# Rows 6 and 7 of the output projection ahead of the first feed-forward products, behind the first transposes of x1; two more slots for y in the last head

## The chip, the cores and the metric

The kernel runs on one core of a Trainium2 chip, as one program. The metric is the device time of one execution in microseconds. Before the change the median of three runs is 1173.84 us (1173.09, 1173.84 and one run of 6371.15 that stands apart). The engines are TensorE (PE for its products, PEld for its weight loads), VectorE (DVE), ScalarE (ACT), GpSimd (POOL, hardly used here) and SyncE (SP), which issues all DMAs.

## The reference

One layer of a hybrid block, for one sequence of 1024 positions and a model width of 1024, in float32:

```python
h = hybrid_mixer(x, ...)                  # three branches, concatenated, @ w_out
x = layer_norm(ALPHA * x + h, ln1_g, ln1_b)          # x1
h = jnp.square(jax.nn.relu(x @ w_up)) @ w_down       # feed-forward, width 4096
x = layer_norm(ALPHA * x + h, ln2_g, ln2_b)
...
return jnp.concatenate([y_conv, y_ml, y_da], axis=-1) @ w_out      # end of hybrid_mixer
```

`y_conv` (256 columns) is a causal depthwise convolution of 31 taps with a layer norm; `y_ml` (256 columns) is a chunked mLSTM; `y_da` (512 columns, 4 heads of 128) is differential attention: two softmax maps for each head, one subtracted from the other, times v, with an RMS norm. The part that the change touches is the product of the concatenated branches with `w_out`, its layer norm (x1 is the result), and the start of the feed-forward part.

## The kernel before, in words

**Precision.** Every large product is made of three: an operand is split into a high part (a ScalarE copy to a rounded format) and a low part (a VectorE subtract), and high*high, high*low and low*high are added up in PSUM. `split` (L145) is that pair of instructions. In the profile, `hi` and `lo` are split weights or inputs, `yh` and `yl` a split row block of y, `wth` and `wtl` split attention weights.

**Stages.** First the input projections, with the convolution and the mLSTM beside them; then four heads of attention, one after another; then the feed-forward part as products of a seven-product (Strassen-like) scheme: P1 to P7, over 16 pairs of 128-column blocks of `w_up` (`up(s, p)`, L1100), and after that `w_down`. The sequence is cut in eight blocks of 128 rows, called row 0 to row 7 here (`tb` in the code).

**The output projection** runs in two passes, since the last heads are late. The branch outputs go to eight DRAM tiles `ydram`, one for each 128 columns. The first pass (`row1`) takes column blocks 0 to 4, adds ALPHA*x and leaves its sums in eight tiles `acc`. The second pass (`row2`, L1074) takes blocks 5, 6 and 7, that is heads 1, 2 and 3. For one row, `get_y` (L857) loads three blocks of `ydram` to `yraw` and splits it to `yh` and `yl`; `row` (L872) then makes 18 products of 512 columns (two halves, three blocks, three products each) into two tiles of the PSUM pool `ps_mm`, which has two banks, adds each half to `acc` on VectorE (L893) and normalises the row: L899, L805 to L811, L904. It stores the result to `zdram`.

**The last head.** `attention(3, ..., fill)` works in four groups g of two row blocks. Scores go to the pool `ps_s`, transposed weights and outputs to `ps_t`, four banks and two; they belong to the attention and are given back at L1092, after which the pool `ps_f` has the six banks. In each group `fill(g)` (L1076) places other work: for g = 1, 2, 3 the rows 2g-2 and 2g-1 of the second pass, and at g = 3 also the first half of the transposes of x1. Group g writes 256 rows of `ydram[7]`, so rows 2g and 2g+1 can be loaded after it; rows 6 and 7 only after the whole head.

**x1.** The feed-forward part needs x1 transposed. `x1_half(t4, ...)` (L981) does it for rows 4*t4 to 4*t4+3: 32 transposes of 128x128 on TensorE into eight banks taken two at a time, each bank read out by ScalarE (L994) or VectorE (L996) into the tiles `xr`. `x1_split` makes the split operands B11 and B21 out of the first half; the others (T1 to T4, B22) are sums with the second half. P1 needs B11, P2 needs B21. The second half of the transposes stands behind the products P1 and P2 of pairs 0 and 1 (L1320).

**Weights.** `w_load(s)` loads two tiles of 512 KB of `w_up`, `w_sums(s)` makes sums x and y out of them, `w_split(s, key)` splits w1, x, y or w2. The last head is preceded by `wo2` (the split of w_out blocks 5 to 7), w_load(0), w_sums(0), w_split(0, "w1") and w_load(1) (L1068 to L1073).

**What sets the order.** Instructions get a priority number when they are written down. `lane(k)` (L88) gives numbers from k million on, so a low lane goes first: 1 for loads, splits and evictions, 2 for the attention, 5 for weights, 6 for products of the rows, 7 for the first transposes; code after L1306 counts from 8 million. When the program is built, each engine's instructions are put in one fixed order, by priority among those that can go; at run time each engine follows its order and waits on semaphores. A lower-priority instruction can thus be put ahead of a higher one that cannot go yet.

**Slots.** SBUF is cut in 47 slots of 128 x 1056 float32. The class `Slots` (L54) hands them out first in, first out: `alloc` takes the slot that was given back longest ago, `free` puts one at the end of the queue, in the order of the code. A new tile in a slot must wait until everything that used the old one is done. From L920 on one ring `F` serves weights, y and x1. Slots are counted by the code, so which tile follows which in a slot can be read off by hand. Before the last head F has 23 free slots: wo2 takes nine and gives three back, w_load(0) takes two, w_sums(0) two, w_split(0, "w1") two and gives one back, w_load(1) two. Ten are left for the rows. After the last head the slots of the attention's ring G join F.

Of the kernel before, what the change touches and what calls it, by code (L numbers as in the profile page):

```python
# [10 lines left out]
F32 = mybir.dt.float32  # L11
# [6 lines left out]
P = 128  # L18
# [79 lines left out]
def mixer_block(ctx: ExitStack, tc: tile.TileContext, a: dict, out: bass.AP):  # L98
# [5 lines left out]
    X = Slots(spool, range(0, 16))  # L104
# [3 lines left out]
    lane = Lanes(tc)  # L108
# [5 lines left out]
    def tr(out, in_, k=P):  # L114
        nc.tensor.transpose(out, in_, ident[:k, :k])  # L115

    def load(out, in_):
        nc.sync.dma_start(out=out, in_=in_)
# [36 lines left out]
    ps_mm = ctx.enter_context(tc.tile_pool(name="ps_mm", bufs=2, space=bass.MemoryType.PSUM))  # L155
# [683 lines left out]
    early = [load_split(W, a["w_out"][kb], D) for kb in range(NEARLY)]  # L839
# [10 lines left out]
    acc = []  # L850
    ydv = [y.rearrange("p (t j) -> p t j", j=P) for y in ydram]

    def out_proj(kbs, first, wo, yring):

        n, ys = len(kbs), {}

        def get_y(tb, ln):  # L857
            with ln(1):
                ring = yring(tb)
                raw = ring.alloc(F32, "yraw")  # L860
                for j, kb in enumerate(kbs):
                    load(raw[:, j * P:j * P + P], ydv[kb][:, tb, :])
                yh, yl = ring.alloc(F32R, "yh"), ring.alloc(F32R, "yl")
                split(raw[:, :n * P], yh[:, :n * P], yl[:, :n * P])
                ring.free(raw)
                if first:
                    xa = (W if tb < NW - 2 * NEARLY else X).alloc(F32, "acc")
                    load(xa[:, :D], a["x"][tb])
                    acc.append(xa)
            ys[tb] = ring, yh, yl  # L870

        def row(tb, ahead=(), ln=lane):  # L872
            for t in ahead:
                get_y(t, ln)
            ring, yh, yl = ys[tb]
            mv = small.tile([P, 6], F32, tag="mvf", name="mvf")
            for nh in range(2):
                cs = slice(nh * 512, nh * 512 + 512)
                with ln(6):
                    ps = ps_mm.tile([P, 512], F32, name="mm")  # L880
                    for j in range(n):
                        ks = slice(j * P, j * P + P)
                        h, l = wo[j]
                        mm(ps, yh[:, ks], h[:, cs], j == 0, False)
                        mm(ps, yh[:, ks], l[:, cs], False, False)
                        mm(ps, yl[:, ks], h[:, cs], False, j == n - 1)
                with ln(1):
                    z = acc[tb][:, cs]
                    if first:
                        dve.scalar_tensor_tensor(out=z, in0=z, scalar=ALPHA, in1=ps, op0=ALU.mult,  # L890
                                                 op1=ALU.add)
                    else:
                        dve.scalar_tensor_tensor(out=z, in0=ps, scalar=1.0, in1=z, op0=ALU.mult,  # L893
                                                 op1=ALU.add, accum_out=mv[:, nh:nh + 1])
            ring.free(yh, yl)
            if not first:
                with ln(6):
                    z = acc[tb][:, :D]
                    dve.tensor_scalar(out=mv[:, 5:6], in0=mv[:, 0:1], scalar1=mv[:, 1:2],  # L899
                                      scalar2=-1.0 / D, op0=ALU.add, op1=ALU.mult)  # L900
                    junk = yring(tb).alloc(F32, "junk")
                    row_scale(z, mv, junk[:, :D])
                    yring(tb).free(junk)
                    act.activation(z, z, AF.Identity, scale=mv[:, 2:3], bias=mv[:, 4:5])  # L904
                    load(zdram[tb], z)

        return row

    zdram = [dram.tile([P, D], F32, name=f"z{i}") for i in range(TB)]
    row1 = out_proj([0, 1, 2, 3, 4], True, early, lambda tb: X)  # L910
    for tb in range(TB):
        if tb == 0:
            early += [load_split(X, a["w_out"][kb], D) for kb in range(NEARLY, 5)]
# [6 lines left out]
    F = Slots(spool, [])  # L920
# [24 lines left out]
    def bank(of_mm=False):  # L945

        if of_mm:
            return ps_mm.tile([P, 512], F32, name="mm")
        return ps_f.tile([P, 512], F32, tag="f", name="f", bufs=6)
# [26 lines left out]
    xraw, xq = {}, {}  # L976
# [4 lines left out]
    def x1_half(t4, two_banks):  # L981

        for i in range(2):
            xraw[i, t4] = [F.alloc(F32, "xr") for _ in range(2)]
        for kb in (0, 4, 2, 6):
            t_ = two_banks()
            for k in range(2):
                for j in range(4):
                    tr(t_[k][:, j * P:j * P + P],
                       acc[4 * t4 + j][:, (kb + k) * P:(kb + k) * P + P])  # L990
                o = xraw[kb // 4, t4][kb % 4 // 2][:, css[k]]
                g_, b_ = l1g[:, kb + k:kb + k + 1], col(PC_L1B + kb + k)
                if k == 0:
                    act.activation(o, t_[k], AF.Identity, scale=g_, bias=b_)  # L994
                else:
                    dve.tensor_scalar(out=o, in0=t_[k], scalar1=g_, scalar2=b_, op0=ALU.mult,  # L996
                                      op1=ALU.add)

    def x1_split(name, raw, keep=False):

        xq[name] = [halves_of(t, keep) for t in raw]
# [29 lines left out]
    def w_load(s):  # L1031
        w1, w2 = F.alloc(F32, "w1"), F.alloc(F32, "w2")
        load(w1[:, :1024], a["w_up"][s])
        load(w2[:, :1024], a["w_up"][s + NS])
        wt[s] = dict(w1=w1, w2=w2, kept=False)
# [13 lines left out]
    def w_split(s, key, keep=False):  # L1049
        w = wt[s]  # L1050
        raw = w[key]
        if key == "w2":
            both = F.alloc(F32R, "w2")
            split(raw[:, H1], both[:, H0], both[:, H1])
            F.free(raw)
            w["P4"] = both[:, H0], both[:, H1]
            w["P4t"] = (both,)
            return
        hi, lo = halves_of(raw, keep)
        w["kept"] = keep  # L1060
        n0, n1 = dict(w1=("P1", "P2"), x=("P5", "P6"), y=("P7", "P3"))[key]
        w[n0], w[n1] = (hi[:, H0], lo[:, H0]), (hi[:, H1], lo[:, H1])
        w[dict(w1="P2", x="P5", y="P3")[key] + "t"] = hi, lo
# [4 lines left out]
    with lane(5):  # L1068
        wo2 = [load_split(F, a["w_out"][kb], D, False) for kb in (5, 6, 7)]
        w_load(0)  # L1070
        w_sums(0)
        w_split(0, "w1")
        w_load(1)  # L1073
    row2 = out_proj([5, 6, 7], False, wo2, lambda tb: F)  # L1074

    def fill(g):  # L1076

        if g > 0:
            row2(2 * g - 2, (2 * g - 2, 2 * g - 1))
            row2(2 * g - 1)  # L1080
        if g == 3:
            with lane(7):
                x1_half(0, lambda: [ps_mm.tile([P, 512], F32, name="mm") for _ in range(2)])
                F.free(*acc[0:4])
                x1_split("B11", xraw[0, 0], True)
                x1_split("B21", xraw[1, 0], True)
                w_split(1, "w1", True)

    with lane(2):
        attention(3, neglam, dag, None, fill)  # L1090
# [9 lines left out]
    def up(s, p):  # L1100
        h = hd.setdefault(s, {})
        if p in ("P1", "P2", "P5"):
            h["a" if p == "P1" else "b"] = bank(p != "P1")
        ps = h["a" if p in ("P1", "P6", "P7", "P4") else "b"]
        wh, wl = wt[s][p]
        go = mm_on(p)
        for kb in range(4):
            ks = slice(kb * P, kb * P + P)
            xh_, xl_ = xq[BOF[p]][kb // 2]
            cs = css[kb % 2]  # L1110
            go(ps, wh[:, ks], xh_[:, cs], kb == 0, False)
            go(ps, wh[:, ks], xl_[:, cs], False, False)
            go(ps, wl[:, ks], xh_[:, cs], False, kb == 3)
        w_done(s, p)
        if p == "P1":
            h["hp"] = F.alloc(F32, "hp")
            act.copy(h["hp"][:, H0], ps)
        elif p == "P2":
            add(h["hp"][:, H0], h["hp"][:, H0], ps)
        elif p == "P6":  # L1120
            h["hq"] = F.alloc(F32, "hq")
            act.copy(h["hq"][:, H0], ps)
        elif p == "P5":
            act.copy(h["hq"][:, H1], ps)
        elif p == "P7":
            add(h["hq"][:, H1], h["hq"][:, H1], ps)
        elif p == "P3":
            add(h["hq"][:, H0], h["hq"][:, H0], ps)
        else:
            act.activation(h["hp"][:, H1], ps, AF.Relu)  # L1130
# [177 lines left out]
    def here(k):  # L1308
        return nullcontext()

    w_load(2)
    up(0, "P1")
    up(0, "P2")
    row2(6, (6, 7), here)
    row2(7, (), here)
    w_split(0, "x")
    up(1, "P1")
    up(1, "P2")
# [223 lines left out]
```

## Time and profile before

| | |
|---|---|
| median of the runs | 1173.84 us |
| the profiled execution's own time | 1175.76 us |
| its span | 1173.9 us |
| granted TensorE clock, mean | 0.992 |
| TensorE busy | 1140.2 us (97%) |
| VectorE busy | 833.4 us (71%) |
| ScalarE busy | 578.1 us (49%) |
| DMA | 179.86 MB, mean 153 GB/s |

Times in the profile count from the start of the span. A line of the time order has the start, the duration, the engine, the source line, the operation, what is written and read, the shape, and in brackets the idle time before it and who ended it. In the table of stretches a row gives the busy time of each engine in that stretch, with the number of instructions, then the granted clock (1.00 is full), the share of the DMA engines and GB/s. The last head runs until about 505 us, and the feed-forward products begin at about 523 us.

### The profile page before, as it was taken

Reading aid. Unit: us, or ns where it says so; the run is one execution under the profiler, and the core shown is the slowest. Engines: PE = TensorE matmul, PEld = TensorE weight load, DVE = VectorE, ACT = ScalarE, POOL = GpSimd, SP = SyncE. Lnnn points to the kernel's source line nnn. Section 1 sums busy time; section 2 is a strip of 40 time slices with the busy share of each in tenths; the row PEclk is TensorE's granted clock in tenths of the full one; section 3 lists DMA queues with packets and bytes.
Section 4 is the critical chain, followed back from the end, with each engine's and each line's share of the span. In section 5 each row is a group of like instructions: output and inputs, shape, how many; then the busy total and the mean of one; then the engine's idle time right before and its main releaser. Section 6 shows DMA issues by size and latency. Waiting matters only on the chain.

```text
span 1173.9 us, 14934 instructions
## 1 busy us (share of the span) xinstructions
PE 1140.2 (97%) x5630; PEld 933.9 (80%) x5630; DVE 833.4 (71%) x1243; ACT 578.1 (49%) x934; POOL 0.2 (0%) x4
## 2 busy tenths in 40 slices
PE   8999999999999899889999999999999999999996
PEld 6898778878897787667788888888888878888885
DVE  5999658875756537867987677656489676666586
ACT  5212384475665526686655454545544323344561
POOL 0000000000000000000000000000000000000000
PEclk9999999999999999899999999999999999999998
DMA  7202135444635663420275555633894644343331
GB/s 279 71 11 72 37 90 167 154 138 128 192 104 174 211 184 105 161 117 37 101 284 215 189 212 192 215 117 146 302 357 159 218 160 147 124 142 128 97 119 72
DMA packets 81640, 179.86 MB, mean 153 GB/s; under 512 B 7648, under 2 KB 29216, under 8 KB 81568
## 3 DMA queue, kind: packets, MB, share of 16 engines
q1 hardware_dynamic: 81568, 178.91, 45.0%
q8 instruction: 44, 0.72, 0.3%
q14 instruction: 28, 0.23, 0.1%
HBM read 120.12 MB, written 58.72 MB: 152 GB/s over the span
## 4 chain that ended last, share of the span: by engine, by line
PE 83%; DVE 7%; ACT 4%; DMA 3%; issue 1%; SPq 0%; DVEq 0%; ACTq 0%
PE f L940 31%; PE mm L112 25%; PE mm L940 17%; PE s L112 5%; PE t L112 3%; PE t L115 2%; DVE lo L148 1%; ACT hi L147 1%; DVE pp L744 1%; ACT pp L738 1%; DMA vh<-v 1%; DVE acc L963 1%; ACT pp L743 0%; DMA raw<-in_w_out 0%; DVE nm L736 0%
## 5 line engine op out<-in xcount | busy, mean ns | idle before, releaser
L940 PE MATMUL f<-lo,hi 128*128 128x512 f32 x512 | 201.5, 394 | 1.4 <-DVE lo L148 1.3
L940 PE MATMUL f<-hi 128*128 128x512 f32 x512 | 201.9, 394 | 0.8 <-DVE acc L1243 0.5
L940 PE MATMUL f<-hi,lo 128*128 128x512 f32 x512 | 201.2, 393 | 0.0
L940 PE MATMUL mm<-hi 128*128 128x512 f32 x320 | 126.1, 394 | 0.4 <-ACT hi L147 0.4
L940 PE MATMUL mm<-lo,hi 128*128 128x512 f32 x320 | 125.9, 393 | 0.3 <-DVE lo L148 0.3
L940 PE MATMUL mm<-hi,lo 128*128 128x512 f32 x320 | 126.0, 394 | 0.0
L940 PEld LDWEIGHTS f<-hi 128*128 128x128 f32 x512 | 96.5, 188 | 24.0 <-ACT hi L147 1.2
L940 PEld LDWEIGHTS f<-lo,hi 128*128 128x128 f32 x512 | 96.3, 188 | 24.0 <-DVE lo L148 2.6
L940 PEld LDWEIGHTS f<-hi,lo 128*128 128x128 f32 x512 | 96.1, 188 | 22.1 <-DVE lo L148 0.2
L112 PE MATMUL mm<-xh,hi 128*128 128x512 f32 x240 | 95.8, 401 | 5.9 <-ACT xh L147 5.9
L147 ACT CAST hi<-hraw 128x1024 fp32r<-128x1024 f32 x56 | 58.3, 1049 | 85.4 <-DMA hraw<-h 80.2
L148 DVE TENSOR_TENSOR lo<-hraw,hi 128x1024 fp32r<-128x1024 f32 x56 | 68.2, 1223 | 44.2 <-ACT hi L147 41.9
L112 PE MATMUL mm<-xl,hi 128*128 128x512 f32 x240 | 96.1, 400 | 0.0
L112 PE MATMUL mm<-xh,lo 128*128 128x512 f32 x240 | 96.0, 400 | 0.0
L285 DVE SCALAR_TENSOR_TENSOR cacc<-ypad,pc,cacc 128x1024 f32<-128x1024 f32 x60 | 74.2, 1283 | 0.6
L112 PE MATMUL mm<-hi,xh 128*128 128x256 f32 (+1 forms) x256 | 74.1, 289 | 0.0
L112 PE MATMUL mm<-hi,xl 128*128 128x256 f32 (+1 forms) x256 | 73.2, 286 | 0.0
L112 PE MATMUL mm<-lo,xh 128*128 128x256 f32 (+1 forms) x256 | 73.1, 286 | 0.0
L940 PEld LDWEIGHTS mm<-hi 128*128 128x128 f32 x320 | 60.3, 189 | 14.7 <-ACT hi L147 0.8
L940 PEld LDWEIGHTS mm<-lo,hi 128*128 128x128 f32 x320 | 60.2, 188 | 14.4 <-DVE lo L148 0.7
L940 PEld LDWEIGHTS mm<-hi,lo 128*128 128x128 f32 x320 | 60.1, 188 | 13.7
L147 ACT CAST hi<-B 128x1024 fp32r<-128x1024 f32 x36 | 37.6, 1048 | 53.7 <-PE mm L940 24.9
(282 smaller groups left out, 2319.5 us busy)
## 6 DMA issues: line engine op xcount, KB each, us to landing
hraw<-h SPq DMA_DIRECT2D x56, 512.0 KB, 3.4
w<-in_w_up SPq DMA_DIRECT2D x32, 512.0 KB, 4.1
B<-in_w_down SPq DMA_DIRECT2D x32, 512.0 KB, 4.7
h<-hp SPq DMA_DIRECT2D x16, 512.0 KB
h<-hx SPq DMA_DIRECT2D x16, 512.0 KB, 3.0
h<-hq SPq DMA_DIRECT2D x16, 512.0 KB, 3.3
raw<-in_wfm SPq DMA_DIRECT2D x14, 512.0 KB, 3.5
qk<-th SPq DMA_DIRECT2D x8, 512.0 KB
```

The costliest lines, as they stand in the source:

```text
L112: return nc.tensor.matmul(out, lhsT=lhsT, rhs=rhs, start=start, stop=stop)
L115: nc.tensor.transpose(out, in_, ident[:k, :k])
L147: act.copy(hi, src)
L148: dve.tensor_tensor(out=lo, in0=src, in1=hi.bitcast(F32), op=ALU.subtract)
L285: dve.scalar_tensor_tensor(out=av, in0=yp[:, i:i + S], scalar=col(PC_DWW + 31 * c + i), in1=av, op0=ALU.mult, op1=ALU.add)
L738: act.activation(pp[m][:, 0:nk], s_[:, 0:nk], AF.Exp, bias=nm[:, m:m + 1], accum_out=sm[:, m:m + 1])
L744: dve.scalar_tensor_tensor(out=pp[0][:, 0:nk], in0=pp[0][:, 0:nk], scalar=sm[:, 0:1], in1=pp[1][:, 0:nk], op0=ALU.mult, op1=ALU.add)
L940: return nc.tensor.matmul(out, lhsT=lhsT, rhs=rhs, start=start and not more, stop=stop and not more, skip_group_check=more)
L963: dve.tensor_tensor(out=out, in0=p, in1=q, op=ALU.add)
```

## The change: what it does

- `get_y` is cut in two: `fetch` takes the slot and issues the three loads of `yraw`; `get_y` takes the slots of `yh` and `yl` and splits, and fetches first if that was not done. `out_proj` returns `fetch` and `get_y` beside `row`.
- `w_load(1)` no longer stands before the last head but in `fill(3)`, still in lane 5. Twelve slots of F are free for the rows at the start of the head, in place of ten.
- The first transposes of x1, the splits of B11 and B21 and the split of w1 of pair 1 leave `fill(3)`. They stand behind the last head, in the code that counts from 8 million, and the transposes use the six banks of `ps_f` (L949) in place of the two of `ps_mm`.
- The order behind the head was: w_load(2), P1 and P2 of pair 0, rows 6 and 7 with their loads. It is now: loads of y for rows 6 and 7, the transposes, the splits of y for rows 6 and 7, the splits of B11 and B21, w_load(2), row 6, the split of w1 of pair 1, row 7, P1 and P2 of pair 0.

No product, DMA or elementwise instruction is added or removed.

```diff
@@ out_proj
-        def get_y(tb, ln):
+        def fetch(tb):
+            ring = yring(tb)
+            raw = ring.alloc(F32, "yraw")
+            for j, kb in enumerate(kbs):
+                load(raw[:, j * P:j * P + P], ydv[kb][:, tb, :])
+            return ring, raw
+
+        def get_y(tb, ln, fetched=None):
             with ln(1):
-                ring = yring(tb)
-                raw = ring.alloc(F32, "yraw")
-                for j, kb in enumerate(kbs):
-                    load(raw[:, j * P:j * P + P], ydv[kb][:, tb, :])
+                ring, raw = fetched or fetch(tb)
                 yh, yl = ring.alloc(F32R, "yh"), ring.alloc(F32R, "yl")
...
-        return row
+        return row, fetch, get_y
...
         w_load(0)
         w_sums(0)
         w_split(0, "w1")
-        w_load(1)
-    row2 = out_proj([5, 6, 7], False, wo2, lambda tb: F)
+    row2, fetch_y, get_y = out_proj([5, 6, 7], False, wo2, lambda tb: F)
...
         if g == 3:
-            with lane(7):
-                x1_half(0, lambda: [ps_mm.tile([P, 512], F32, name="mm") for _ in range(2)])
-                F.free(*acc[0:4])
-                x1_split("B11", xraw[0, 0], True)
-                x1_split("B21", xraw[1, 0], True)
-                w_split(1, "w1", True)
+            with lane(5):
+                w_load(1)
...
+    last_y = [fetch_y(tb) for tb in (6, 7)]
+    x1_half(0, lambda: (bank(), bank()))
+    F.free(*acc[0:4])
+    for tb, fetched in zip((6, 7), last_y):
+        get_y(tb, here, fetched)
+    x1_split("B11", xraw[0, 0], True)
+    x1_split("B21", xraw[1, 0], True)
     w_load(2)
+    row2(6, (), here)
+    w_split(1, "w1", True)
+    row2(7, (), here)
     up(0, "P1")
     up(0, "P2")
-    row2(6, (6, 7), here)
-    row2(7, (), here)
     w_split(0, "x")
     up(1, "P1")
```

More of the change, by code (lines that the diff above doesn't have):

```diff
@@ L905, in row @@
                     load(zdram[tb], z)
-        return row
+        return row, fetch, get_y
     zdram = [dram.tile([P, D], F32, name=f"z{i}") for i in range(TB)]
-    row1 = out_proj([0, 1, 2, 3, 4], True, early, lambda tb: X)
+    row1, _, _ = out_proj([0, 1, 2, 3, 4], True, early, lambda tb: X)
     for tb in range(TB):
```

## The prediction

> **What bounds the kernel now.** I read the page first, then a table of stretches, then the instructions of TensorE in order of time around the change, and last who ended its waits.
>
> ```profile
> span 1173.9 us, 14934 instructions
> PE 1140.2 (97%) x5630; PEld 933.9 (80%) x5630; DVE 833.4 (71%) x1243; ACT 578.1 (49%) x934; POOL 0.2 (0%) x4
> ...
> PE 83%; DVE 7%; ACT 4%; DMA 3%; issue 1%; SPq 0%; DVEq 0%; ACTq 0%
> ```
>
> TensorE is busy for 97% of the span and carries 83% of the chain that ended last. The change removes no product, so it can win only idle or slowed time of TensorE. The next table (start:end and length, then busy us and instructions of PE, PEld, DVE, ACT, POOL, then the granted clock) says where that is.
>
> ```profile
> 480.00:500.00 20.00, 16.18 (x75) 13.05 (x74) 17.17 (x36) 12.93 (x25) 0.00 (x0) 0.83 0.38 115
> 500.00:515.00 15.00, 15.00 (x67) 12.06 (x66) 9.88 (x33) 11.51 (x23) 0.00 (x0) 1.00 0.31 122
> 515.00:530.00 15.00, 11.46 (x60) 8.29 (x59) 10.87 (x22) 13.24 (x20) 0.00 (x0) 1.00 0.26 106
> 530.00:545.00 15.00, 15.00 (x67) 12.13 (x66) 6.87 (x21) 7.33 (x13) 0.00 (x0) 1.00 0.09 36
> 545.00:590.00 45.00, 43.01 (x197) 33.43 (x195) 44.22 (x52) 31.54 (x39) 0.00 (x0) 1.00 0.28 102
> 590.00:1160.00 570.00, 569.48 (x2466) 463.34 (x2465) 397.12 (x466) 258.45 (x306) 0.00 (x0) 1.00 0.51 180
> ```
>
> From 590 on there is nothing to win: 569.48 of 570 us. There are three places: A, the end of the last head (480 to 500: 3.8 us idle, clock 0.83); B, the first transposes of x1 (515 to 530: 3.5 us idle); C, 545 to 590, with 2.0 us idle where VectorE is full (44.22 of 45).
>
> **Place A.**
>
> ```profile
> 489.74 0.39 PE L112 MATMUL mm<-hi,yl 128*128 128x512 f32 x1
> 492.21 1.44 PE L115 MATMUL t<-cst,pp 128*128 128x128 f32 x8 [2.08 <-DVE pp L744]
> 494.24 0.58 PE L112 MATMUL t<-wth,vh 128*128 128x256 f32 x1 [0.59 <-DVE wtl L148]
> 499.42 0.54 PE L112 MATMUL mm<-hi,yh 128*128 128x512 f32 x1
> ...
> 482.59 1.22 DVE L148 TENSOR_TENSOR lo<-raw,hi 128x1024 fp32r<-128x1024 f32 x1
> 483.83 1.28 SPq L118 DMA_DIRECT2D yraw<-ydram  x3
> 491.98 1.22 DVE L148 TENSOR_TENSOR lo<-w,hi 128x1024 fp32r<-128x1024 f32 x1
> 494.16 0.52 ACT L147 CAST yh<-yraw 128x384 fp32r<-128x384 f32 x1
> 494.91 0.55 DVE L148 TENSOR_TENSOR yl<-yraw,yh 128x384 fp32r<-128x384 f32 x1
> 495.37 1.22 DVE L148 TENSOR_TENSOR lo<-wx,hi 128x1024 fp32r<-128x1024 f32 x1
> ```
>
> Row 1 of the second output projection ends at about 489.97, and TensorE stands still until the attention's last transposes; row 2, the work that could stand there, comes only at 499.42. Its y arrives late because of the ring of slots, which is first in, first out: counted through the code, row 2 gets for yraw the slot of the third w_out raw (split until 483.81, loads at 483.83) and for yh the slot of w1 of pair 0, read until 493.20 by the subtract at 491.98. So yh is written at 494.16.
>
> With w_load(1) gone from before the head, the ring holds 12 free slots in place of 10. Counted again, row 2's yraw, yh and yl get the three w_out raws' slots, all free at 483.81, so its y can be whole by about 486, in time for 489.97. Row 3 pays: its yraw now gets the slot of w1, free at 493.20.
>
> What the gap cost, from rows of normal speed:
>
> ```profile
> 473.53 0.34 PE L112 MATMUL t<-wth,vh 128*128 128x256 f32 x1
> ...
> 475.63 0.45 PE L112 MATMUL mm<-lo,yh 128*128 128x512 f32 x1
> ...
> 517.58 1.09 PE L115 MATMUL mm<-cst,acc 128*128 128x128 f32 x8 [0.46 <-DVE acc L893]
> ...
> 531.36 8.12 PE mm L112 x35
> ...
> DMA to landing us min/median/max: 1.9/2.9/3.4
> ```
>
> Between 473.53 and 475.63 lie 18 products of weights and values, 2.10 us, so the 24 of the last group are worth 2.80; eight transposes 1.09; a row product is 8.12/35 = 0.232, a row of 18 takes 4.18. From 489.97 to 499.42 pass 9.45 us for 1.09 + 2.80: 5.56 are lost, 2.67 as idle and the rest to a slow clock. Afterwards: row 2 until 494.15, transposes until 495.24, the wait for wtl (0.59, kept at 0.6), products until 498.64. Row 3 then starts 4.96 us ahead of 503.60, where row 2 ended before. Row 3's y: slot at 493.20, last of three loads issued 0.85 later, landed 2.9 later, copies 0.52 and 0.55: 498.0, a margin of 0.6. VectorE now has row 2's subtract and eviction around that split of w1, so I take a stall of 0.4. **A: 4.6 gained**, bounds 0 (the order stays) and 5.56.
>
> The clock, row first:
>
> ```profile
> 490.00:492.50 2.50, 0.42 (x4) 0.32 (x4) 2.50 (x5) 0.42 (x1) 0.00 (x0) 1.00 0.66 239
> 492.50:495.00 2.50, 1.91 (x11) 1.51 (x9) 2.33 (x6) 1.91 (x4) 0.00 (x0) 0.55 0.23 61
> 495.00:497.50 2.50, 2.50 (x14) 2.50 (x13) 1.74 (x3) 2.50 (x7) 0.00 (x0) 0.50 0.01 1
> ```
>
> A gap of 2.08 us was followed by about 5 us at half clock. [...]
>
> **Place B.** Before, the first transposes pass through two banks of ps_mm behind row 5, nothing else is ready, and the first product waits for the splits of B11.
>
> ```profile
> 516.52 0.60 PE L115 MATMUL mm<-cst,acc 128*128 128x128 f32 x4
> ...
> 520.70 1.09 PE L115 MATMUL mm<-cst,acc 128*128 128x128 f32 x8 [0.91 <-DVE xr L996]
> ...
> 524.51 0.51 PE L940 MATMUL f<-lo,hi 128*128 128x512 f32 x1 [0.77 <-DVE lo L148]
> ...
> 544.84 3.84 PE L115 MATMUL f<-cst,acc 128*128 128x128 f32 x28
> ...
> 593.99 2.77 PE mm L940 x12
> ```
>
> From 516.52 to 544.84, where the second transposes begin, pass 28.32 us. The work in them: 32 transposes at 3.84/28 = 4.39 (the second set, with six banks, shows this pace), rows 6 and 7 with 36 x 0.232 = 8.35, four products of 12 at 2.77 = 11.08; 23.82 in all, so 4.50 are lost. Afterwards the transposes have the six banks that the attention gave back, and rows 6 and 7, 8.35 us, lie over the splits of B11 and B21 (eight instructions) and of w1 of pair 1. Are these covered?
>
> ```profile
> 508.38 0.69 DVE L893 SCALAR_TENSOR_TENSOR acc<-mm,acc 128x512 f32<-128x512 f32 x1
> ...
> 511.30 0.56 DVE L148 TENSOR_TENSOR yl<-yraw,yh 128x384 fp32r<-128x384 f32 x1
> ...
> 513.50 1.24 ACT L904 ACTIVATE acc<-acc,mvf 128x1024 f32<-128x1024 f32 x1 [1.53 <-DVE mvf L811]
> ...
> 519.84 0.81 DVE L996 TENSOR_SCALAR xr<-mm,l1g,pc 128x512 f32<-128x512 f32 x1 [0.75 <-PE mm L115]
> ...
> 523.23 1.23 DVE L148 TENSOR_TENSOR lo<-xr,hi 128x1024 fp32r<-128x1024 f32 x1
> ```
>
> Row 3 is normalised 513.50 + 1.24 - 508.38 = 6.4 us after its last eviction began, and rows 4 and 5 cover 8.35. B11 and B21 cost VectorE 4 x 1.23 = 4.9 against that 8.35, with four evictions of rows 6 and 7 at 0.69: 7.7, just covered. The new exposed step is y of rows 6 and 7. Their raws are fetched early, but yl of row 6 takes the slot of row 5's yh, free only when row 5 ends, and stands behind the evictions of the transposes if the order follows the code. Then the last eviction (0.81) and yh (0.52) leave TensorE dry for 1.3 us; but before, row 6's y was subtracted at 511.30, well ahead of its place in the code (behind the first products), so a subtract can be slipped in where VectorE is free, and I take half, 0.7. **B: 3.8 gained**, bounds 0 and 4.50.
>
> **Place C and the queues.** The split of x of pair 0 was done before 500 (lo<-wx at 495.37); the ring now hands it the slot of acc0, so it runs after the transposes, 1.23 of VectorE more there, with 1.1 for y of rows 6 and 7 just before. The 8.1 us that VectorE sits idle between 530 and 545 take this first; what spills into 545 to 590 delays TensorE one for one. I take 0.5 lost; bounds 2.3 lost (all of it) and 2.0 gained (C's idle gone, since row 7 ends about 5.5 us of products earlier against the second transposes). w_load(1) is two DMAs of 512 KB; they now wait for row 2's junk and row 3's yh, and their w1 is first split behind row 6, some 17 us later (rows 4 and 5, transposes, row 6: 8.35 + 4.39 + 4.18), against this time to landing of 4.1:
>
> ```profile
> w<-in_w_up SPq DMA_DIRECT2D x32, 512.0 KB, 4.1
> ```
>
> So they cost nothing unless SP stands still. On SP, row 3's loads now wait at the head for the w1 slot; queued behind are the loads for rows 4 and 5, which need row 0's and row 1's junk anyway, and the store of the last y group. The six loads of rows 6 and 7 have rows 4 and 5 and the transposes, 8.35 + 4.39, over them.
>
> **The sum.** 4.6 + 3.8 - 0.5 = 7.9. The profiled execution took 1175.76, with 1.86 outside the span, and would take 1167.9; the median of the runs shown, 1173.84, becomes **1165.9, say 1166**.
>
> **Rivals.** (1) Only B is won: row 2 keeps its place, because the order on TensorE is fixed when the program is built. Against it: its y is ready 8 us sooner. 1173.84 - 3.3 = 1170.5; chance 0.16. (2) Only A is won: y of rows 6 and 7 opens a gap of 2 us or more, the clock halves, and the 24 products that took 5.18 in place of 2.80 (494.24 to 499.42) price that at 2.4: B's gain is gone, 1169.7; 0.12. (3) The 32 transposes do not hold the clock up: the run of 4.39 us would be followed by one drop, 2.4 more, 1168.3. The table has clock 1.00 over 515 to 530 with 32 of them and little else for 6 us, so 0.04. [...] (4) The change does not do what it says: as row 6's subtract at 511.30 shows, instructions were already moved against the code's order, and the new order may come out much like the old. 1173.5; 0.08. (5) Slower: SP stands at row 3's loads because the subtract of w1 falls behind row 2's evictions on VectorE, which themselves wait for TensorE. Each us beyond the margin of 0.6 costs one, and 2.4 more once the gap passes 2 us. A's 4.96 and the 3.3 of B and C are used up when it starts after about 498.5, in place of 491.98; at 502 the result is 1177.3. For it: the split is queued below everything of the attention. Against it: its inputs are there, and VectorE was not full over that stretch (17.17 of 20). 0.08.
>
> **How the numbers follow.** The forecast has 0.50 and its own range 1163 to 1169. Rivals 1 to 4 lie below 1174, 0.40 together. The range 1162.5 to 1174 has at the lower end all of A, all of B and 1.3 of C; it leaves out rival 5 and a remainder of 0.02. About 2%, 23.5 us, is what a measurement of this kernel can tell from no change. The idle time of all three places is 9.4, so faster by 2% has 0.01; slower by 2% would need three times rival 5, 0.02; within 2% 0.97.
>
> **What would show it.** Right: no gap above 1 us on TensorE between row 1's end and the last head's end, clock 1.00 there, row 2's products ahead of the last weights-and-values products; the first transposes at one pace on bank f, then rows 6 and 7 at once, then the first product with no wait on lo. Wrong: a wait of row 3's products for yl, a clock below 1 after a new gap, SP idle behind a yraw load, or more than 2.5 us idle from 540 to 585.

## The result and the profile after

The changed kernel takes 1168.43 us (median of four runs, 1167.34 to 1169.96) against 1173.54 for the kernel before (also four runs, with the one of 6371.15 among them): a ratio of 0.995, 95% interval 0.9938 to 0.9962. The interval leaves the run that stands apart out, and is 4.5 to 7.3 us, 5.9 in the middle. The profiled execution took 1168.21.

The first lines of the page of the kernel after, with its chain by engine:

```profile
span 1166.4 us, 14925 instructions
PE 1136.2 (97%) x5630; PEld 930.8 (80%) x5630; DVE 830.8 (71%) x1243; ACT 577.5 (50%) x934; POOL 0.2 (0%) x4
...
PE 85%; DVE 7%; DMA 3%; ACT 3%; issue 2%; SPq 0%; DVEq 0%; ACTq 0%
```

TensorE's busy time fell by 4.0 us with the same 5630 products, mostly since products at half clock last longer: the last 24 products of weights and values took 5.18 us before (494.24 to 499.42) and take 2.78 here (491.20 to 493.98), and the clock of 480 to 500 went from 0.83 to 1.00, which is (1.00 - 0.83) x 20 = 3.4; the rest of what the span lost is idle time. The chain has TensorE at 85% where it had 83%. The span is 7.5 us shorter, which is more than the runs give. Part of it is not the change's. One product of the order in time shows it; the order of the instructions of TensorE, VectorE and ScalarE ahead of it is the same in both kernels. TensorE in the kernel before, with the product near 582 that waits for `hq` behind place C:

```profile
390.34 0.76 PE L112 MATMUL mm<-hi,yh 128*128 128x512 f32 x1 [2.75 <-DVE tl L148]
...
582.65 0.47 PE L940 MATMUL f<-hi,w 128*128 128x512 f32 x1 [0.66 <-DVE hq L963]
```

The same product in the kernel after:

```profile
388.01 0.77 PE L112 MATMUL mm<-hi,yh 128*128 128x512 f32 x1 [2.48 <-DVE tl L148]
```

It starts 2.33 us sooner in the execution after. Over the twelve traces of this study its start spreads from 388.01 to 390.34. All comparisons of traces below therefore count from this product. From it, the second transposes of x1 begin 148.67 us later (536.68) where it was 154.50 (544.84): 5.8 gained. Up to the product that waits for `hq` (574.16 and 582.65) it is 6.2.

The same stretches as before, in the kernel after (busy us and instructions of PE, PEld, DVE, ACT, POOL, then granted clock, DMA share, GB/s):

```profile
480.00:500.00 20.00, 17.62 (x94) 13.79 (x95) 15.80 (x35) 12.55 (x25) 0.00 (x0) 1.00 0.27 92
500.00:515.00 15.00, 14.99 (x77) 12.32 (x77) 9.64 (x38) 12.45 (x23) 0.00 (x0) 1.00 0.72 237
515.00:530.00 15.00, 13.45 (x60) 10.71 (x61) 14.87 (x32) 14.16 (x21) 0.00 (x0) 1.00 0.18 73
530.00:545.00 15.00, 14.99 (x82) 12.42 (x81) 9.21 (x16) 11.19 (x18) 0.00 (x0) 1.00 0.18 72
545.00:590.00 45.00, 43.21 (x183) 33.57 (x182) 42.80 (x52) 27.71 (x34) 0.00 (x0) 1.00 0.37 134
```

The clock is 1.00 throughout, and 515 to 530 has 1.6 us idle where it had 3.5. But 480 to 500 is still 2.4 us idle. TensorE in order of time says where:

```profile
480.51 0.50 PE L112 MATMUL mm<-lo,yh 128*128 128x512 f32 x1 [1.40 <-DVE lo L148]
482.33 0.96 PE L115 MATMUL t<-cst,pp 128*128 128x128 f32 x7 [0.62 <-DVE sm L741]
484.10 0.50 PE L112 MATMUL mm<-lo,yh 128*128 128x512 f32 x1 [0.34 <-DVE lo L148]
485.62 0.50 PE L112 MATMUL mm<-hi,yh 128*128 128x512 f32 x1 [0.33 <-DVE acc L897]
...
491.20 0.29 PE L112 MATMUL t<-wth,vh 128*128 128x256 f32 x1
...
493.98 0.44 PE L112 MATMUL mm<-hi,yl 128*128 128x512 f32 x1
...
498.99 0.88 PE L115 MATMUL f<-cst,acc 128*128 128x128 f32 x6 [0.55 <-ACT acc L908]
499.72 0.50 PE L112 MATMUL mm<-hi,yh 128*128 128x512 f32 x1
...
504.00 0.82 PE L115 MATMUL f<-cst,acc 128*128 128x128 f32 x6
...
512.96 2.57 PE L115 MATMUL f<-cst,acc 128*128 128x128 f32 x20
...
518.02 0.50 PE L112 MATMUL mm<-hi,yl 128*128 128x512 f32 x1 [1.55 <-DVE yl L148]
...
536.68 3.98 PE L115 MATMUL f<-cst,acc 128*128 128x128 f32 x32
...
574.16 0.47 PE L944 MATMUL f<-hi,w 128*128 128x512 f32 x1 [0.61 <-DVE hq L967]
```

The gap of 2.08 us ahead of the last transposes of the attention is gone: row 2 now stands there, on both sides of the last 24 products of weights and values (491.20 to 493.98). Two things are new. Idle time now lies some 10 us earlier, where row 0 of the second pass waits for the splits of w_out (1.40 and 0.34, the `lo`) and around them. And 12 of the 32 first transposes no longer stand behind row 5: six are put after row 2 and six after row 3 (498.99 and 504.00). They are those of rows 0 and 1, one for each of the six banks. Why they fit there, VectorE's instructions say, in order of time:

```profile
492.16 1.22 DVE L148 TENSOR_TENSOR lo<-w,hi 128x1024 fp32r<-128x1024 f32 x1
493.29 0.33 DVE L903 TENSOR_SCALAR mvf<-mvf 128x1 f32<-128x1 f32 x2
...
497.46 0.56 DVE L148 TENSOR_TENSOR yl<-yraw,yh 128x384 fp32r<-128x384 f32 x1 [0.69 <-ACT yh L147]
...
498.97 0.69 DVE L897 SCALAR_TENSOR_TENSOR acc<-mm,acc 128x512 f32<-128x512 f32 x1 [0.95 <-ACT acc L908]
...
503.77 0.69 DVE L897 SCALAR_TENSOR_TENSOR acc<-mm,acc 128x512 f32<-128x512 f32 x1 [1.46 <-ACT acc L908]
```

ScalarE's normalisation of row 1, in the kernel after:

```profile
502.51 1.23 ACT L908 ACTIVATE acc<-acc,mvf 128x1024 f32<-128x1024 f32 x1
```

SP's queue in the kernel after, whose first loads of y for row 3 are among these nine:

```profile
493.45 4.88 SPq L118 DMA_DIRECT2D yraw<-ydram  x9
```

An eviction is VectorE's addition of a finished half row to `acc`. The first one of row 3 (503.77) starts when the normalisation of row 1 ends (502.51 + 1.23 = 503.74), though the two touch different rows of `acc`. What they share is the small tile `mvf` for a row's sums: its pool has two buffers, so row t takes the one of row t-2. While the eviction waits, the two banks of `ps_mm` are full, and the rows' products wait too. The transposes on six banks of their own can go in that time. That row 2 waits in the same way (498.97) has a second side: the last eviction of row 0 ended at 486.17, but VectorE begins row 0's normalisation only at 493.29, in the place that the fixed order gives it. No run here put it earlier.

### The profile page after: what moved, and what is told of

Its sections match the earlier page's. It is cut to its first block, busy times and chain, and to the rows that moved or that the text cites. A ratio compares the mean times of both kernels' runs of the same rounds, so it can differ in the third digit from the quotient of the medians.

```text
span 1166.4 us, 14925 instructions
## 1 busy us (share of the span) xinstructions
PE 1136.2 (97%) x5630; PEld 930.8 (80%) x5630; DVE 830.8 (71%) x1243; ACT 577.5 (50%) x934; POOL 0.2 (0%) x4
## 4 chain that ended last, share of the span: by engine, by line
PE 85%; DVE 7%; DMA 3%; ACT 3%; issue 2%; SPq 0%; DVEq 0%; ACTq 0%
PE f L944 32%; PE mm L112 26%; PE mm L944 17%; PE s L112 5%; PE t L112 3%; PE t L115 2%; DVE lo L148 1%; DMA kh<-qk 1%; ACT pp L738 1%; DVE acc L967 1%; DMA xraw<-in_xT 0%; DMA vh<-v 0%; DMA hraw<-h 0%; DVE nm L736 0%; DVE pp L744 0%
```

## The experiments

Each ratio is against the kernel before, on the same chip, with its 95% interval. Four points cut each trace in three stretches: the product at 390, the end of row 5's products, the beginning of the second transposes, and the first product that waits for `hq` (574.16 in after). The first stretch holds place A, the second is place B, the third is what place C delays. Where 12 transposes lie ahead of row 5's end, 1.65 us (12 x 4.39/32, the prediction's price) is moved from the first stretch to the second. No kernel here leaves computation out.

### The slots alone

```diff
-        w_load(1)                      # before the last head
     def fill(g):
...
         if g == 3:
+            with lane(5):
+                w_load(1)
             with lane(7):
                 x1_half(0, ...)        # transposes, splits stay as before
```

> Only the slots: w_load(1) moves into the third group's fill, so the rows of the last head find 12 free slots in place of 10; the first transposes, and rows 6 and 7, stay where they were. As forecast (place A alone, 4.6 us): about 1169. By the traces of before and after, in which 2.3 of the 7.5 us that separate the two profiles lie ahead of any changed instruction and a new wait of 1.4 us for a split of w_out stands at 480: 2.5 to 3 us, about 1170.5. If the slots do nothing by themselves and the order behind the head did it all: 1173.5. Clock between 490 and 500 us: 1.00 by the first two, about 0.66 by the last.

Measured: 0.9995 (0.9986 to 1.0003), 0.6 us. TensorE in this kernel, in order of time:

```profile
482.20 0.50 PE L112 MATMUL mm<-lo,yh 128*128 128x512 f32 x1 [1.39 <-DVE lo L148]
...
501.43 0.50 PE L112 MATMUL mm<-hi,yh 128*128 128x512 f32 x1 [1.28 <-DVE acc L893]
...
507.10 0.51 PE L112 MATMUL mm<-hi,yh 128*128 128x512 f32 x1 [1.22 <-DVE acc L893]
```

VectorE at the first of the two waits, and below it the normalisation on ScalarE:

```profile
500.68 0.69 DVE L893 SCALAR_TENSOR_TENSOR acc<-mm,acc 128x512 f32<-128x512 f32 x1 [0.95 <-ACT acc L904]
```

```profile
499.40 1.24 ACT L904 ACTIVATE acc<-acc,mvf 128x1024 f32<-128x1024 f32 x1
```

The slots do what the prediction said: no gap at 490, and the clock over 480 to 500 is 1.00 in place of 0.83. But two new waits of 1.28 and 1.22 us stand behind it, and the eviction that ends the first, row 2's, begins when the normalisation of row 0 ends (499.40 + 1.24). Here nothing else is ready for TensorE, so 2.5 us go back. The trace gives 0.63 for place A, 0.05 for B.

### The rows alone

```diff
         w_split(0, "w1")
+        w_load(1)                      # as in the kernel before: ten slots
...
-        if g == 3:
-            with lane(5):
-                w_load(1)              # the rest of the change stays
```

> Only the order behind the head: transposes on six banks, then rows 6 and 7, then the first products; w_load(1) is back in front of the last head, so the rows have 10 slots as before. As forecast (B and C, 3.3 us): 1170.2. By the trace of after (28.3 us between row 5's end and the second transposes became 25.4): 3 us, 1170.5. If the two parts need each other: 1173. The gap of 2 us at 490 and the clock of about 0.66 between 490 and 500 should be there again.

Measured: 0.9953 (0.994 to 0.9966), 5.5 us: nearly the whole change. Its stretch at the end of the head, and TensorE:

```profile
480.00:500.00 20.00, 17.34 (x86) 13.09 (x85) 16.81 (x37) 12.89 (x26) 0.00 (x0) 0.91 0.25 88
```

```profile
483.92 0.96 PE L115 MATMUL t<-cst,pp 128*128 128x128 f32 x7 [2.56 <-DVE sm L740]
...
501.83 0.88 PE L115 MATMUL f<-cst,acc 128*128 128x128 f32 x6 [0.83 <-ACT acc L908]
...
520.71 0.50 PE L112 MATMUL mm<-hi,yl 128*128 128x512 f32 x1 [1.28 <-DVE yl L148]
```

The gap of 2 us at 490 was expected to be there again. With ten slots, as before, it is gone as well. A gap of 2.56 us stands at 484 in its place, and the clock over 480 to 500 is 0.91, where the kernel before had 0.83, so place A still gains 1.75 by the trace. That is the difference of the clock: (0.91 - 0.83) x 20 = 1.6. The head's instructions were not edited. With the work of lane 7 gone from `fill(3)` the fixed order inside the head came out otherwise (on VectorE the sums `wy` of pair 0 now stand ahead of the split of w_out); that the one caused the other is argued, not shown.

### y of rows 6 and 7 ahead of the transposes

```diff
     last_y = [fetch_y(tb) for tb in (6, 7)]
+    for tb, fetched in zip((6, 7), last_y):
+        get_y(tb, here, fetched)
     x1_half(0, lambda: (bank(), bank()))
     F.free(*acc[0:4])
-    for tb, fetched in zip((6, 7), last_y):
-        get_y(tb, here, fetched)
```

> The changed kernel with one step exchanged: the splits of y of rows 6 and 7 stand ahead of the first transposes in the code, so that they are put ahead of the transposes' evictions on VectorE. In the changed kernel TensorE waits 1.55 us for the low part of row 6's y. If that subtract is late only because of the four evictions in front of it: the wait is gone, 1.5 us faster than the changed kernel, about 1167. If VectorE, full in that stretch (14.87 of 15 us), only passes the delay on to the splits of B11 and B21: the same as the changed kernel, 1168.4. If its slots or loads hold it: the same too, with the wait still named yl.

Measured: 0.9931 (0.9919 to 0.9943), 8.1 us, about 2 better than the change, though the two intervals overlap at the edge (0.9938 to 0.9943). The stretch that held the wait for yl:

```profile
515.00:530.00 15.00, 15.00 (x67) 12.16 (x66) 14.71 (x32) 14.05 (x25) 0.00 (x0) 1.00 0.18 71
```

TensorE is full there. Place B gains 4.8 in place of 2.95. In the changed kernel the subtract for row 6 stands behind the evictions of the transposes, as these lines of VectorE in the kernel after show:

```profile
514.34 0.80 DVE L1000 TENSOR_SCALAR xr<-f,l1g,pc 128x512 f32<-128x512 f32 x1
...
515.13 2.24 DVE L1000 TENSOR_SCALAR xr<-f,l1g,pc 128x512 f32<-128x512 f32 x3
...
517.41 0.56 DVE L148 TENSOR_TENSOR yl<-yraw,yh 128x384 fp32r<-128x384 f32 x1
```

Four evictions stand ahead of it, and row 6 cannot go on before it. VectorE works without a break from 512.79 to that subtract, so it is its order that made row 6 wait; with y first no wait for yl is left on TensorE.

### The transposes through two banks

```diff
-    x1_half(0, lambda: (bank(), bank()))
+    x1_half(0, lambda: (bank(True), bank(True)))     # the two banks of ps_mm
```

> The changed kernel with the first transposes passed through the two banks of ps_mm, as before the change, in place of six of ps_f. If the six banks carry part of the gain of place B: the waits for evictions among the transposes come back, 2.3 us in the trace of before (0.46, 0.47, 0.91, 0.43), so about 1170.7. If rows 6 and 7 behind the transposes carry it all, because ScalarE and VectorE are the limit there: 1168.4.

Measured: 0.9977 (0.9967 to 0.9987), 2.7 us: more than half of the gain is lost. TensorE in this kernel:

```profile
500.53 0.50 PE L112 MATMUL mm<-hi,yh 128*128 128x512 f32 x1 [1.28 <-DVE acc L897]
...
514.33 1.27 PE L115 MATMUL mm<-cst,acc 128*128 128x128 f32 x8 [0.41 <-DVE acc L897]
...
518.20 2.99 PE L115 MATMUL mm<-cst,acc 128*128 128x128 f32 x16 [0.91 <-DVE xr L1000]
```

The wait of 1.28 for the eviction is bare again, as with the slots alone, and the transposes wait for their own evictions once more. Six banks thus pay twice: at the transposes, and ahead of them by letting twelve go early. For the second, the bare waits speak (1.28, and 0.37 at 505.34, in place of 0.55); of the 1.7 us that place A loses against the change in the table below, a drop of the clock at 482 (shown at the end) would by itself make up as much.

### Six buffers for the rows' sums: with the slots alone, with the kernel before

```diff
-            mv = small.tile([P, 6], F32, tag="mvf", name="mvf")
+            mv = small.tile([P, 6], F32, tag="mvf", name="mvf", bufs=6)
```

The same in the other two places that use the tag.

> The slots alone again (w_load(1) late, order behind the head as before), and the tile mvf of a row's sums and factors gets six buffers in place of two. With the slots alone the gap of 2 us at 490 was gone and TensorE then stood 1.28 and 1.22 us at 501 and 507 behind evictions that begin when ScalarE's L904 of the row two before ends: the two buffers of mvf. If that is what gave the gain of place A back: both waits gone, 2.5 to 3 us faster than before, ratio about 0.9975. If ScalarE and VectorE are simply late there: ratio 0.9995 as with the slots alone, and the evictions wait for something else.

> The kernel before, with six buffers of mvf and nothing else changed: the control for the slots with six buffers (ratio 0.9963). If the two buffers matter only once row 2 can start at 490, because before that the rows run without a wait: ratio 1.000. If the buffers alone gave that gain: 0.9965.

Measured: slots with buffers 0.9963 (0.995 to 0.9976), 4.3 us, against 0.6 for the slots alone. The kernel before with buffers: 0.9982 (0.9973 to 0.9991), 2.1 us. In the first, from row 2 to the end of row 5 no wait is left on TensorE; the next after those at 480 to 485 is this:

```profile
484.71 0.50 PE L112 MATMUL mm<-hi,yh 128*128 128x512 f32 x1 [0.32 <-DVE acc L893]
...
511.13 1.09 PE L115 MATMUL mm<-cst,acc 128*128 128x128 f32 x8 [0.70 <-DVE acc L893]
```

So the slots' gain went into the waits on the two buffers: they are gone, and the intervals of 0.9995 and 0.9963 lie apart. On top of the buffers the slots are worth 2.2 us, though there the intervals overlap a little (0.9973 to 0.9976). The buffers win something by themselves, since in the kernel before, too, row 5's first eviction waits for row 3's normalisation. VectorE in the kernel before:

```profile
514.78 0.69 DVE L893 SCALAR_TENSOR_TENSOR acc<-mm,acc 128x512 f32<-128x512 f32 x1 [1.13 <-ACT acc L904]
```

TensorE in the kernel before with six buffers, where TensorE's idle time from the transposes to the first products adds up to 1.7 in place of 3.5:

```profile
491.63 1.06 PE L115 MATMUL t<-cst,pp 128*128 128x128 f32 x8 [2.08 <-DVE pp L744]
...
515.95 1.30 PE L115 MATMUL mm<-cst,acc 128*128 128x128 f32 x8 [0.35 <-DVE acc L893]
```

The gap of 2.08 at the end of the head stays: the buffers do nothing for place A's idle time. The clock behind it is 0.63 and 0.69 over the two rows of 2.5 us from 492.5 on, where the kernel before had 0.55 and 0.50, and 0.91 in place of 0.83 over 480 to 500. That shorter drop is worth (0.91 - 0.83) x 20 = 1.6, more than the 1.0 that place A gains in this trace, so the 1.0 is not shown to come from the buffers.

### Three versions with y first

y first with six buffers:

> The kernel with the y splits ahead of the transposes (ratio 0.9931), and six buffers of mvf. There the first transposes of x1 already stand in the waits for evictions (0.55 us left). If those transposes fill the waits fully: no change, 0.993. If the waits of VectorE for ScalarE's L904 still hold up what follows (the splits of B11 and B21): up to 1 us more, 0.992.

y first, and the six slots that the attention's ring hands over put at the head of the queue instead of its end, so that the splits of w_out get others:

```diff
-    X.give(G.take(6))
+    X.q.extendleft(reversed(G.take(6)))
```

> The kernel with the y splits ahead of the transposes (0.9931), and the six slots that the attention's ring gives up put at the front of the queue in place of the end, so that the first two blocks of w_out get slots that are free about 50 us earlier. Its trace has waits of 1.39, 0.62, 0.34 and 0.32 us between 479 and 485, named by splits of w_out blocks and the evictions behind them. If the late slots cause them: 2 to 2.5 us less, ratio about 0.991. If the order of the splits on VectorE causes them: 0.993.

y first with `w_load(1)` back ahead of the head (ten slots):

> The order behind the head with the y splits ahead of the transposes, but w_load(1) in front of the last head, so 10 slots. Set beside 0.9931 with 12 slots it shows what the two slots are worth once the first transposes can stand in the waits for evictions. If they are worth the 2.8 us that place A showed in the profile of the changed kernel: ratio about 0.9955. If they are worth nothing, as they were alone: 0.993, with a gap near 484 or 490 and a lower clock in its place.

Measured: 0.9929 (0.9914 to 0.9945), 0.9929 (0.9913 to 0.9945) and 0.9954 (0.9938 to 0.997). Six buffers add nothing once the transposes fill the waits: with the buffers all 32 stand together behind row 5, without them twelve go early, and the time is the same. The moved slots do remove the waits for w_out, but the clock over 480 to 500 is 0.91, and TensorE in that kernel has this wait in their place:

```profile
481.28 0.50 PE L112 MATMUL mm<-hi,yh 128*128 128x512 f32 x1 [3.14 <-ACT yh L147]
```

Without the two slots, y first is worth nothing that these runs can tell against the rows alone (0.9954 and 0.9953). By the traces place B does gain 1.5 more (4.7 against 3.2), but place A about 1 less (0.8 against 1.75, with the clock behind 390 taken off as below); why, these runs do not show. With y first, the slots are worth 0.0023, or 2.7 us, though the two intervals overlap at the edge.

### The changed kernel again

> The changed kernel once more, beside the control on the same chip, to set it against the version with the y splits first (0.9931) with a narrower interval. If the wait of 1.55 us for the low part of row 6's y is worth what it shows: ratio 0.9945 to 0.995. If the first measurement was low by chance: 0.993. In its trace the instructions ahead of 390 us, which no edit touches, should lie within a spread of about 2 us of those of the other kernels, with no relation to the edits.

Measured: 0.9947 (0.9935 to 0.996). The change repeats.

### All together

Us gained against the kernel before, by the traces, and the ratio of the runs:

| kernel | A | B | C | sum | ratio |
|---|---|---|---|---|---|
| the change | 2.9 | 2.95 | 0.3 | 6.2 | 0.9950 |
| the change again | 3.1 | 2.95 | 0.3 | 6.4 | 0.9947 |
| slots alone | 0.6 | 0.05 | 0.0 | 0.7 | 0.9995 |
| rows alone | 1.75 | 3.2 | 0.3 | 5.3 | 0.9953 |
| transposes on two banks | 1.2 | 1.05 | 0.35 | 2.6 | 0.9977 |
| slots, six buffers | 5.95* | 0.2 | 0.0 | 6.15* | 0.9963 |
| before, six buffers | 1.0 | 2.15 | 0.0 | 3.2 | 0.9982 |
| y first | 4.6* | 4.8 | 0.3 | 9.7* | 0.9931 |
| y first, six buffers | 3.4 | 5.1 | 0.3 | 8.8 | 0.9929 |
| y first, moved slots | 2.9 | 5.3 | 0.3 | 8.5 | 0.9929 |
| y first, ten slots | 2.5* | 4.7 | 0.3 | 7.5* | 0.9954 |

In the three with a star the clock did not drop behind the product at 390, as it did in the others. (In place A the clock over 480 to 500 was 0.83 before, 0.91 with the rows alone, two banks, moved slots, ten slots and before with six buffers, and 1.00 in the rest.) The drop is worth about 1.7 us, (1 - 0.57) x 2.5 + (1 - 0.75) x 2.5 from the rows shown at the end, and has nothing to do with the edit. Less 1.7, the sums of these three are 4.45, 8.0 and 5.8, against 4.3, 8.1 and 5.4 by the ratios. Of the whole table only the kernel before with six buffers stands more than 1 us from its ratio (3.2 against 2.1); the shorter drop of the clock in its one trace is enough for that.

## Why the prediction was right, and where it was wrong

The size and the sign held: 7.9 us were forecast, 5.9 were measured, and 1168.4 lies inside the range. The forecast took 23.5 us for the least that a measurement of this kernel can tell from no change; the interval here, 4.5 to 7.3 us, tells 5.9 from none. That the profiled execution came out at 1168.21, next to the 1167.9 of the sum, is partly luck: 2.33 us of it are the product at 390.

**A, 4.6 forecast, 2.9 found.** The reading of the ring was right: row 2 does stand in the gap. The margin of row 3 was right too: its y was whole at 497.46 + 0.56 = 498.0, as worked out, although SP stood at its loads until 493.45, when the split of w1 (492.16 + 1.22) had let go of their slot. Two steps failed.

First, the step "Row 3 then starts 4.96 us ahead" looked at row 3's y and at no other thing that row 3 and row 4 need. Their products need a free bank, and the evictions of rows 2 and 3, which free one, waited for the small tile `mvf` of the row two back. In the slots alone that took 2.5 us back; in the change the early transposes hide most of it, and 0.55 stays. The row at 514.78 was in the trace of before, and was not read.

Second, the sum took the idle time ahead of 489.97 as it was. Before, the waits for the splits of w_out were 0.56 and 0.58; after, four waits there make 1.40 + 0.62 + 0.34 + 0.33 = 2.69. In all, the idle time from the first of these waits to the end of row 5 fell only from 0.56 + 0.58 + 2.08 + 0.59 = 3.81 to 2.69 + 0.55 = 3.24, and ahead of them, from the product at 390 on, it grew by about as much (from 1.55 to 2.17, by the waits of more than 0.03 us). What is left is the half clock, 5.56 - 2.67 = 2.9 us in the prediction's sum, and the trace gives 2.9. So place A paid by the clock and not by its idle time.

The step also gave A to the slots. The rows alone win 1.75 there. By the ratios the two slots are worth 0.4 to 0.7 us in the change (0.9950 and 0.9947 against 0.9953), less than these intervals can tell from nothing.

**B, 3.8 forecast, 2.95 found.** The limit of 4.50 was a little low: the versions with y first come to 4.7 to 5.3. Of the work in it, the 32 transposes were priced at 4.39 and took 3.90 where they stand together (y first with six buffers, 512.62). The term that was mis-sized most is the wait for y of row 6. It was taken at 0.7, half of 1.3, because a subtract might be slipped in; it measured 1.55. That 4.50 - 1.55 is just the 2.95 found owes something to the low limit. The splits of B11 and B21 are covered, as forecast: the first product with B11 (523.45, among row 6's and 7's) has no wait. That six banks pay twice was not foreseen; B would have been about 1 without them.

**C, -0.5 forecast, +0.3 found.** The split of x of pair 0 did move to 518.20, as forecast, but cost nothing there: from the second transposes to the product that waits for `hq` pass 574.16 - 536.68 = 37.48 us, where it was 582.65 - 544.84 = 37.81.

**The rivals.** Only B: the rows alone come close to it in time, but not as meant, since the order in the head did not stay. Only A through a gap of 2 us at y of row 6: the mechanism is real, the gap 1.55, the clock stayed 1.00. Transposes that do not hold the clock up: 20 in a row (512.96, 2.57 us) and then row 6 ran at 1.00. With y first and six buffers 32 stood in a row for 3.90 us, and the clock was 1.00 behind them too. Order unchanged: no. SP standing at row 3's loads: it stood, and cost nothing, because the y came within its margin.

**The signs named.** The clock of 1.00 and row 2's place came as named. No gap above 1 us stands between row 1's end and the last head's end, as named, and the first products with B11 do not wait. That the transposes would go at one pace, with rows 6 and 7 at once behind them, did not hold: 12 went early, and row 6 waited.

**What stays open.** Why the fixed order inside the head changes when work of a lower priority leaves it (rows alone, moved slots) was not tried by itself. Nor was what lets the waits for w_out grow from 1.14 to 2.69 when the slots change; moving the slots exchanged them for one of 3.14. The traces show that the two slots reach far: with them TensorE's order differs from that of the kernel before from 427 us on, some 60 us ahead of place A, and with the rows alone only from 482 on.

## What to carry to other kernels

Where a wait is closed, ask of the work that now starts earlier what every buffer of it waits for, the smallest too: a tile of six columns in two buffers held a pipeline of rows two rows back, and that wait stood in the trace before the change. Work with banks of its own is worth most where it can stand in waits that nobody planned for; and a load's split that the next product needs belongs ahead of evictions that nothing needs yet. The version with y first is faster than the kernel before, 0.9931 (0.9919 to 0.9943); against the changed kernel its trace shows the 1.85 us of place B, while the intervals of the two overlap at the edge.

## What the runs showed of the hardware

The clock does not follow from a gap's length alone. These are the rows behind the product at 390, in the kernel before (gap 2.75) and below it in the version with y first (gap 2.44):

```profile
390.00:392.50 2.50, 2.16 (x5) 1.81 (x6) 1.52 (x3) 0.49 (x1) 0.00 (x0) 0.57 0.88 357
392.50:395.00 2.50, 2.50 (x10) 1.94 (x10) 0.98 (x2) 0.36 (x2) 0.00 (x0) 0.75 0.90 211
```

```profile
390.00:392.50 2.50, 2.50 (x12) 1.88 (x11) 0.87 (x2) 0.84 (x2) 0.00 (x0) 1.00 1.01 290
392.50:395.00 2.50, 2.50 (x16) 2.05 (x15) 1.30 (x3) 1.25 (x4) 0.00 (x0) 1.00 0.77 270
```

A gap of 2.48, in the kernel after, was followed by a drop; one of 2.99 was not, as TensorE with the slots and six buffers shows:

```profile
389.60 0.47 PE L112 MATMUL mm<-hi,yh 128*128 128x512 f32 x1 [2.99 <-DVE tl L148]
```

The product behind it took 0.47 us, and those that follow it ran at full pace; in the kernels before and after it took 0.76 and 0.77. And with the transposes on two banks, waits of 1.39 and 0.63, the same that the kernel after passes at 1.00, were followed by half clock. TensorE in that kernel, then its stretch:

```profile
482.19 1.73 PE L115 MATMUL t<-cst,pp 128*128 128x128 f32 x7 [0.63 <-DVE sm L741]
```

```profile
482.50:485.00 2.50, 2.50 (x11) 2.21 (x10) 2.09 (x3) 2.00 (x4) 0.00 (x0) 0.50 0.28 115
```

The seven transposes took 1.73 us in place of the 0.96 of the rows alone (483.92).

At the product at 390 a gap stands in each of the twelve traces, 2.36 to 3.06 us long, in a part that no edit touches. A drop followed it in nine of them, the shortest and the longest among them (2.36 in the kernel before with six buffers, where the clock was 0.65 over 390 to 392.5; 3.06 with the rows alone, where it was 0.50), and none in three: 2.43 in y first with ten slots, 2.44 in y first, 2.99 with the slots and six buffers, all with 1.00 over 390 to 395. The 2 us from which rivals 2 and 5 let the clock halve are thus no bound: these three are longer and cost no clock, and the waits of 1.39 and 0.63 are each shorter and did. What decides it, these runs do not show. Nor do they show why the gap of 2.08 at the end of the head cost more in the kernel before than with six buffers, 0.83 and 0.91 over 480 to 500. One execution's gain from a gap that is closed carries an uncertainty of one such drop, 1.7 us here.
